# A hybrid trunk layer on one core: four-tile visits for the second modulation, two late groups, one-operation table levels, and first loads in another order

## The chip, the cores and the metric

The kernel runs on one core of a Trainium2 chip. The metric is the device time of one execution in microseconds (us), as the median over several runs. One further execution was recorded by the hardware profiler; all rows below come from it.

The engines are named as in the trace: PE multiplies matrices (PEld is its weight load), DVE works on vectors, ACT applies functions and copies, POOL is the general engine, and SP issues nearly all loads, in the order of its program.

## The reference

```python
cond = silu(c)                                   # c: 1 x 2048
mod = cond @ w_mod + b_mod                       # 2048 x 12288
sh1, sc1, gt1, sh2, sc2, gt2 = split(mod, 6)
h = rms_norm(x, g_pre_mix) * (1 + sc1) + sh1     # x: 256 x 2048
y = hybrid_mixer(h, ...)   # h @ w_in, then three branches:
      # SSM of 2048 complex states with a GLU, dilated attention of 24 heads,
      # a gated short convolution; each is projected to 2048 columns, scaled by a
      # sigmoid gate of h @ w_in, summed, and multiplied by w_o
x = x + gt1 * rms_norm(y, g_post_mix)
h = rms_norm(x, g_pre_ffn) * (1 + sc2) + sh2
y = conv_ffn(h, ...)       # h @ w_up (11264 columns), width-3 convolution, silu(a) * b, @ w_down
x = x + gt2 * rms_norm(y, g_post_ffn)
```

All values are float32. Half 0 of the modulation is the pair (sh1, sc1), half 1 the pair (sh2, sc2).

## The kernel before

**Products.** Each float32 operand is split in a high and a low part: ACT copies the high one (L72), DVE subtracts for the low one (L73). `mm3` (L125 to L128) makes three matmuls of one product. Weights come as tiles of 128x1024 (512 KB) into the four slots of the pool `raw`; `next_weights` keeps two tiles loaded and split ahead of the one in use (`AHEAD = 2`). A slot is free for the next load when both halves of the split have read it.

**Stages, in time from the span's start.** Start (to 48.7 us): load `x` transposed as `xt` in four tiles, spread `silu(c)` over all partitions (`cond_row`, two tiles), sum the squares of `xt` on PE (`ssps`), take the root on ACT and the reciprocal with a Newton step on DVE (`rstd`), make the modulation of the first two column groups, and from them `h` and its split, `hh` and `hl` (`h_pair`). Then four passes of two column groups over `w_in` for SSM and attention (`inps`, to 285 us), the convolution branch (`cps`, to 386 us), three gate branches of 16 output tiles `f` each (`gps`: branch 0 and 1 to about 660 us, then the GLU, branch 2 from about 690 to 787 us), the output projection (`ops<-mh`, to 876 us), a middle part that normalises and transposes (to 892 us), the FFN's upward products (`ups`, to 1390 us) and its second output projection (to 1637 us).

**Modulation.** Each half has eight groups of 256 scale and 256 shift columns. A group on DVE (`mod_half`) reads eight 128x1024 weight tiles; each is multiplied with `cond_row` and summed by one operation (L193). Half 0 puts its tiles in the pool `bo` (six slots, two of them held by `cond_row` and two at first by the loaded `c`), half 1 in `raw`, that is, among the weights. `PE_MOD` names the groups made on PE instead (groups 4 to 7 of half 1): `mod_rows_pe` takes two tiles, one in `mraw` and one in `raw`, for four matmuls of 32x512 output (L154) between the matmuls of the main work. We call this a visit. A group has four visits, and then a transposition on PE (L177) and a sum on DVE. The post-mix gate is made by `mod_gate`, whose tiles go into the pool `dx` (five slots).

**Order of the work.** Side work is written as generators; a `Filler` steps each by a rate per tick, two ticks in an `f`. The order of each engine's program is that in which these steps fall. In the convolution and in gate branches 0 and 1, `fs` is the SSM and `m2` the second modulation: groups 0 to 3 as DVE rows, then 4 to 7 as visits. `mod_gate` runs in gate branch 2 and in the output projection.

**SSM tables.** `table` makes cosine and sine rows `T` of 256 steps by four doublings for each of 16 state blocks: one scaled copy on ACT (L700) and two operations on DVE (L703, L707) in each. The angles come from POOL operations in `ssm_params`, at the start.

## Time and profile before

| what | value |
|---|---|
| median of three runs (1638.06, 1642.01, 1641.61) | 1641.61 us |
| the profiled execution | 1646.62 us |
| its span, first to last instruction | 1644.6 us |
| PE busy | 97% of the span |
| DVE, ACT, POOL busy | 74%, 50%, 3% |
| bytes moved by DMA | 388.52 MB, mean 236 GB/s |

The span is what the views below are drawn over; about 2 us of the execution lie outside it. A busy share is over the whole span and says nothing of a single stage.

### The profile page before, as it was taken

Reading aid. Unit: us, or ns where it says so; the run is one execution under the profiler, and the core shown is the slowest. Engines: PE = TensorE matmul, PEld = TensorE weight load, DVE = VectorE, ACT = ScalarE, POOL = GpSimd, SP = SyncE. Lnnn points to the kernel's source line nnn. Section 1 sums busy time; section 2 is a strip of 40 time slices with the busy share of each in tenths; the row PEclk is TensorE's granted clock in tenths of the full one; section 3 lists DMA queues with packets and bytes.
Section 4 is the critical chain, followed back from the end, with each engine's and each line's share of the span. In section 5 each row is a group of like instructions: output and inputs, shape, how many; then the busy total and the mean of one; then the engine's idle time right before and its main releaser. Section 6 shows DMA issues by size and latency. Waiting matters only on the chain.

```text
span 1644.6 us, 26089 instructions
## 1 busy us (share of the span) xinstructions
PE 1587.6 (97%) x10112; PEld 1400.8 (85%) x10112; DVE 1217.2 (74%) x1854; ACT 814.7 (50%) x1223; POOL 52.0 (3%) x102
## 2 busy tenths in 40 slices
PE   5899999999999999999998999999999999999997
PEld 3898998889888889999887888888888888888886
DVE  5889987887777788787757778877788777444444
ACT  4553434664445554544446555555555555343342
POOL 8021000000000000000000000000000000000000
PEclk8899999999999999999999999999999999999999
DMA  7988975777776665888864777767777665556563
GB/s 264 367 316 281 372 264 172 252 252 251 266 269 240 211 230 165 299 304 321 291 200 137 227 238 235 232 215 231 235 236 230 201 190 188 185 191 191 187 188 125
DMA packets 107120, 388.52 MB, mean 236 GB/s; under 512 B 11890, under 2 KB 12018, under 8 KB 106996
## 3 DMA queue, kind: packets, MB, share of 16 engines
q1 hardware_dynamic: 105268, 380.96, 69.5%
q10 hardware_dynamic: 1728, 5.90, 1.0%
q8 instruction: 79, 1.29, 0.3%
q14 instruction: 45, 0.37, 0.1%
HBM read 384.71 MB, written 2.10 MB: 235 GB/s over the span
## 4 chain that ended last, share of the span: by engine, by line
PE 81%; DVE 8%; DMA 7%; ACT 3%; issue 2%; SPq 0%; DVEq 0%; ACTq 0%
PE ups L901 20%; PE ups L902 10%; PE ops L127 7%; PE ops L126 7%; PE ops L128 7%; PE gps L126 5%; PE gps L128 5%; PE gps L127 5%; PE inps L126 4%; PE inps L128 4%; PE inps L127 4%; DVE lo L73 3%; DMA raw<-in_wB 2%; DMA raw<-in_wmod_t 2%; DMA raw<-in_wA 1%
## 5 line engine op out<-in xcount | busy, mean ns | idle before, releaser
L73 DVE TENSOR_TENSOR lo<-raw,hi 128x1024 fp32r<-128x1024 f32 x520 | 635.4, 1225 | 290.1 <-ACT hi L72 287.8
L72 ACT CAST hi<-raw 128x1024 fp32r<-128x1024 f32 x520 | 543.0, 1047 | 555.2 <-PE ops L128 172.9
L901 PE MATMUL ups<-h2p,hi 128*128 128x512 f32 x1408 | 495.3, 394 | 0.1
L902 PE MATMUL ups<-h2p,lo 128*128 128x256 f32 x1408 | 398.1, 283 | 0.0
L901 PEld LDWEIGHTS ups<-h2p,hi 128*128 128x128 f32 x1408 | 264.4, 188 | 61.6 <-ACT hi L72 0.5
L902 PEld LDWEIGHTS ups<-h2p,lo 128*128 128x128 f32 x1408 | 264.7, 188 | 0.6 <-issue 0.5
L128 PE MATMUL gps<-hh,lo 128*128 128x256 f32 x768 | 217.2, 283 | 4.1 <-DVE lo L73 4.1
L126 PE MATMUL gps<-hh,hi 128*128 128x256 f32 x768 | 220.0, 286 | 0.2 <-ACT hi L72 0.2
L127 PE MATMUL gps<-hl,hi 128*128 128x256 f32 x768 | 216.8, 282 | 0.0
L126 PEld LDWEIGHTS gps<-hh,hi 128*128 128x128 f32 x768 | 145.5, 189 | 15.7 <-issue 8.9
L128 PEld LDWEIGHTS gps<-hh,lo 128*128 128x128 f32 x768 | 145.3, 189 | 4.9 <-DVE lo L73 4.9
L126 PE MATMUL inps<-hh,hi 128*128 128x256 f32 x448 | 128.1, 287 | 22.1 <-ACT hh L72 14.8
L127 PEld LDWEIGHTS gps<-hl,hi 128*128 128x128 f32 x768 | 145.4, 189 | 0.2 <-issue 0.2
L126 PE MATMUL ops<-hi,ah 128*128 128x512 f32 x352 | 138.9, 395 | 0.0
L127 PE MATMUL ops<-lo,ah 128*128 128x512 f32 x352 | 138.9, 395 | 0.0
L128 PE MATMUL ops<-hi,al 128*128 128x512 f32 x352 | 138.9, 395 | 0.0
L128 PE MATMUL inps<-hh,lo 128*128 128x256 f32 x448 | 128.2, 287 | 1.9 <-DVE lo L73 1.7
L127 PE MATMUL inps<-hl,hi 128*128 128x256 f32 x448 | 127.4, 285 | 0.3 <-DVE hl L73 0.3
L126 PEld LDWEIGHTS inps<-hh,hi 128*128 128x128 f32 x448 | 85.9, 193 | 22.9 <-ACT hh L72 15.2
L128 PEld LDWEIGHTS inps<-hh,lo 128*128 128x128 f32 x448 | 85.6, 191 | 3.2 <-DVE lo L73 3.1
L127 PEld LDWEIGHTS inps<-hl,hi 128*128 128x128 f32 x448 | 86.0, 192 | 0.8 <-DVE hl L73 0.6
L193 DVE SCALAR_TENSOR_TENSOR mraw<-mraw,cond_row 128x1024 f32<-128x1024 f32 x64 | 79.1, 1254 | 0.7 <-DMA mraw<-in_wmod_t 0.6
(248 smaller groups left out, 2325.8 us busy)
## 6 DMA issues: line engine op xcount, KB each, us to landing
raw<-in_wup SPq DMA_DIRECT2D x176, 512.0 KB, 4.2
raw<-in_wB SPq DMA_DIRECT2D x120, 512.0 KB, 4.6
raw<-in_wdn SPq DMA_DIRECT2D x88, 512.0 KB, 3.5
raw<-in_wA SPq DMA_DIRECT2D x80, 512.0 KB, 5.2
mraw<-in_wmod_t SPq DMA_DIRECT2D x64, 512.0 KB, 5.9
raw<-in_wmod_t SPq DMA_DIRECT2D x32, 512.0 KB, 4.8
dx<-in_wmod_g SPq DMA_DIRECT2D x32, 512.0 KB, 6.7
raw<-in_wo SPq DMA_DIRECT2D x32, 512.0 KB, 4.5
```

Source lines behind the costliest of these rows:

```text
L72: marks["act"] = nc.scalar.copy(hi, src)
L73: nc.vector.tensor_sub(lo, src, hi)
L126: nc.tensor.matmul(dst, wh, ah, start=first, stop=False)
L127: nc.tensor.matmul(dst, wh, al, start=False, stop=False)
L128: nc.tensor.matmul(dst, wl, ah, start=False, stop=last)
L193: nc.vector.scalar_tensor_tensor(w, w, 1.0, cond_row[kc], ALU.mult, ALU.mult, accum_out=mp2[:, q, kc : kc + 1])
L901: nc.tensor.matmul(ps, wh[:, c], hp, start=kt == 0, stop=False)
L902: nc.tensor.matmul(ps[:, 0], wl[:, c], hp[:, 0], start=False, stop=kt == KT - 1)
```

## The change

Five edits are made together.

1. `PE_MOD` of half 1 is (3, 4, 5) instead of (4, 5, 6, 7). A PE group is now made in two visits of eight matmuls: four tiles per visit, of which two come in halves into four tiles `mq` (in the pool `uv`, whose space the SSM's `M1` and `M2` give up: six buffers each instead of eight), one into `mraw`, one into `raw`. There is a step of the generator after each tile.
2. Half 1 is called in three pieces: groups 0 to 2 during the convolution, groups 3 to 5 during gate branches 0 and 1 at a rate of 1 step per `f`, groups 6 and 7 as DVE rows during gate branch 2 (a quarter step per `f`) and, behind `mod_gate`, in the output projection (`rest`), where what is left is drained before the last quarter.
3. `table` scales the two rows of `T` in two ACT operations, one with the negated sine (`NPS`), and needs one DVE operation for each doubling.
4. The angles become a generator in three parts: the reciprocal of the denominator first, the rest after the root and after the first `h`.
5. The first loads are asked for in another order: `c` in four pieces of 512, the first modulation group's tiles between those of `xt`, two weight tiles ahead of the second group's.

```diff
@@ -27,7 +27,7 @@
 GATE_ORDER = (2, 1, 0)
 AHEAD = 2
 LAG = False
-PE_MOD = ((), (4, 5, 6, 7))
+PE_MOD = ((), (3, 4, 5))
 
 V_C = 0
 V_GPM = 16
@@ -144,20 +144,28 @@
         return w
 
     def mod_rows_pe(src_of, res):
-        condp = marks["condp"]
+        condp, quarter = marks["condp"], marks["quarter"]
         ps = psA.tile([P, 512], F32, tag="A", name="modps")
-        for j in range(4):
-            ws = [mod_raw(i, src_of(2 * j + i)) for i in range(2)]
-            yield
-            for q in range(4):
-                kt = 4 * j + q
+        for j in range(2):
+            parts = []
+            for i in range(4):
+                src = src_of(4 * j + i)
+                if i < 2:
+                    for k in range(2):
+                        t = quarter[2 * i + k]
+                        nc.sync.dma_start(t, src[:, 512 * k : 512 * k + 512])
+                        parts.append(t)
+                else:
+                    w = mod_raw(i, src)
+                    parts += [w[:, 0:512], w[:, 512:1024]]
+                yield
+            for q in range(8):
+                kt = 8 * j + q
+                c = kt % 4
                 nc.tensor.matmul(
-                    ps[32 * q : 32 * q + 32], condp[:, kt],
-                    ws[q // 2][:, 512 * (q % 2) : 512 * (q % 2) + 512],
+                    ps[32 * c : 32 * c + 32], condp[:, kt], parts[q],
                     start=kt < 4, stop=kt >= KT - 4,
                 )
-            if j < 3:
-                yield
         acc = sp.tile([P, 512], F32, tag="junk", name="acc")
         nc.scalar.copy(acc, ps)
         res.append(acc)
@@ -286,6 +294,8 @@
                 for t in range(2):
                     mms(j, w, t)
             last = [next_weights(min(AHEAD, nj - 1 - j)) for j in range(cut, nj)]
+            if filler is not None and n == 2:
+                filler.finish()
             if n == 2:
                 dummy = cp.tile([P, 1], F32, tag="dummy", name="dummy")
                 nc.scalar.activation(dummy, ss[:, 0, 0:1], AF.Sqrt)
@@ -312,9 +322,17 @@
...
-        def ssm_params():
+        params = []
+
+        def ssm_angles():
             AR, AI = V[:, V_AR : V_AR + 16], V[:, V_AI : V_AI + 16]
             dt, th, kk, t1, t2, mag = (sm(n) for n in ("dt", "th", "kk", "t1", "t2", "mag"))
+            rden = sm("rden")
+            nc.gpsimd.tensor_mul(rden, AR, AR)
+            nc.gpsimd.tensor_mul(t2, AI, AI)
+            nc.gpsimd.tensor_add(rden, rden, t2)
+            nc.vector.reciprocal(rden, rden)
+            yield
...
@@ -328,6 +346,7 @@
...
             nc.gpsimd.tensor_scalar(th, th, 3.1415925, -3.1415925, ALU.min, ALU.max)
+            yield
...
@@ -338,24 +357,22 @@
...
-            nc.gpsimd.tensor_mul(t1, AR, AR)
-            nc.gpsimd.tensor_mul(t2, AI, AI)
-            nc.gpsimd.tensor_add(t1, t1, t2)
-            nc.vector.reciprocal(t1, t1)
...
+            NPS = mp.tile([P, 4, 16], F32, tag="NPS", name="NPS")
+            nc.gpsimd.tensor_scalar(NPS, PS[:, 4:8], -1.0, None, ALU.mult)
...
@@ -393,7 +410,8 @@
...
-        mag, PC, PS, SC, SS, fr, fi = ssm_params()
+        angles = ssm_angles()
+        next(angles)
         nc.scalar.activation(cond, V[:, V_C : V_C + KT], AF.Silu)
         ident = mp.tile([P, P], F32, tag="ident", name="ident")
...
@@ -404,20 +422,23 @@
...
-        c1 = [mp.tile([1, 1024], F32, tag="bo", name="c1", bufs=6) for _ in range(2)]
-        for i in range(2):
-            nc.sync.dma_start(c1[i], crow[:, 1024 * i : 1024 * i + 1024])
+        c1 = [mp.tile([1, 512], F32, tag="uv", name="c1", bufs=20) for _ in range(4)]
+        for i in range(4):
+            nc.sync.dma_start(c1[i], crow[:, 512 * i : 512 * i + 512])
...
         xt = [big("xt") for _ in range(4)]
-        for i in range(4):
-            nc.sync.dma_start(xt[i], xT[:, 4 * i : 4 * i + 4])
+        first = mod_half(0, 0, scale1, shift1, V_GPM, V_BMOD + 16, V_BMOD, LAG)
+        for i in range(7):
+            next(first)
+            if i >= 3:
+                nc.sync.dma_start(xt[i - 3], xT[:, 4 * (i - 3) : 4 * (i - 3) + 4])
+        drain(first)
...
@@ -428,10 +449,12 @@
                     ps[:, :S], oinv, sq[:, k], start=(i + k == 0), stop=(i + k == 8)
                 )
         rstd = tp.tile([P, S], F32, tag="rstd", name="rstd")
-        nc.scalar.activation(rstd, ps[:, :S], AF.Sqrt, bias=eps[:, 0:1])
+        root = nc.scalar.activation(rstd, ps[:, :S], AF.Sqrt, bias=eps[:, 0:1])
         nc.vector.reciprocal(rstd, rstd)
         nt = tp.tile([P, S], F32, tag="nt", name="nt")
         newton(rstd, nt, ps[:, :S])
+        with tc.issue_after(root.ins):
+            next(angles)
 
         hhq = [big("hh", F32R) for _ in range(4)]
         hlq = [big("hl", F32R) for _ in range(4)]
@@ -579,7 +602,12 @@
...
         fa = Filler(attention_all(), 0.0)
-        drain(prepare(GROUPS[0]))
+        h_pair(0)
+        with tc.issue_after(marks["act"].ins):
+            drain(angles)
+        mag, PC, PS, NPS, SC, SS, fr, fi = params[0]
+        prefetch(2)
+        drain(prepare(GROUPS[0][1:]))
         for gi, grp in enumerate(GROUPS):
             n = len(grp)
             nxt = GROUPS[gi + 1] if gi + 1 < len(GROUPS) else []
@@ -686,8 +714,8 @@
             gqh = mp.tile([P, 4, S], F32R, tag="bo", name="gqh", bufs=6)
             gql = mp.tile([P, 4, S], F32R, tag="bo", name="gql", bufs=6)
             ssm_st["g"] = (gq, gqh, gql)
-            M1s = [mp.tile([P, 2, S], F32, tag="uv", name="M1", bufs=20) for _ in range(8)]
-            M2s = [mp.tile([P, 2, S], F32, tag="uv", name="M2", bufs=20) for _ in range(8)]
+            M1s = [mp.tile([P, 2, S], F32, tag="uv", name="M1", bufs=20) for _ in range(6)]
+            M2s = [mp.tile([P, 2, S], F32, tag="uv", name="M2", bufs=20) for _ in range(6)]
             Ts = {}
 
             def table(s):
@@ -698,14 +726,13 @@
                     m = 1 << e
                     tt = zp.tile([P, 2, P], F32, tag="tt", name="tt", bufs=2)
                     nc.scalar.activation(
-                        tt[:, :, :m], T[:, :, :m], AF.Copy, scale=PS[:, e, s : s + 1]
+                        tt[:, 0, :m], T[:, 1, :m], AF.Copy, scale=NPS[:, e - 4, s : s + 1]
+                    )
+                    nc.scalar.activation(
+                        tt[:, 1, :m], T[:, 0, :m], AF.Copy, scale=PS[:, e, s : s + 1]
                     )
                     nc.vector.scalar_tensor_tensor(
-                        T[:, 0, m : 2 * m], T[:, 0, :m], PC[:, e, s : s + 1], tt[:, 1, :m],
-                        ALU.mult, ALU.subtract,
-                    )
-                    nc.vector.scalar_tensor_tensor(
-                        T[:, 1, m : 2 * m], T[:, 1, :m], PC[:, e, s : s + 1], tt[:, 0, :m],
+                        T[:, :, m : 2 * m], T[:, :, :m], PC[:, e, s : s + 1], tt[:, :, :m],
                         ALU.mult, ALU.add,
                     )
                 Ts[s] = T
...
@@ -802,20 +829,23 @@
...
-        def mods2():
-            for g in range(8):
+        def mods2(groups):
+            for g in groups:
                 yield from mod_half(1, g, scale2, shift2, V_GPF, V_BMOD + 64, V_BMOD + 48)
 
         fill = lambda g: Filler(g, 0.0)
-        m2 = fill(mods2())
+        m2 = fill(mods2((0, 1, 2)))
         run(conv_branch(), (fa, 3.1), (m2, 2))
         fa.finish()
+        m2.finish()
...
+        marks["quarter"] = [mp.tile([P, 512], F32, tag="uv", name="mq", bufs=20) for _ in range(4)]
         fs = fill(ssm_all(zp))
-        run(gate_branch(0, 2), (fs, 0.7), (m2, 2))
-        run(gate_branch(1, 1), (fs, 0.75), (m2, 1.5))
+        m2 = fill(mods2((3, 4, 5)))
+        run(gate_branch(0, 2), (fs, 0.7), (m2, 1.0))
+        run(gate_branch(1, 1), (fs, 0.75), (m2, 1.0))
         fs.finish()
         m2.finish()
         zs.close()
@@ -831,8 +861,15 @@
             return w
 
         mg = fill(mod_gate(0, gg, load_late, 3))
-        run(gate_branch(2, 0), (mg, 1.5))
-        mg.rate = 1.0
+        m2 = fill(mods2((6, 7)))
+        run(gate_branch(2, 0), (mg, 1.4), (m2, 0.25))
+
+        def rest():
+            yield from gen_g
+            yield from gen_m
+
+        gen_g, gen_m = mg.gen, m2.gen
+        mg = Filler(rest(), 1.0)
 
         ss = cp.tile([P, 2, 4], F32, tag="ss", name="ss1", bufs=2)
         x1 = []
```

On DVE's program at the start, the rows from the reciprocal `rstd` to the first `scale1` are these in the kernel before (L193 multiplies a modulation tile, `mp2_302` is group 0, `mp2_338` group 1):

```order
L432 RECIPROCAL rstd_262<-rstd_262 128x256
L193 SCALAR_TENSOR_TENSOR mraw_315,mp2_302<-mraw_315,cond_row_207 128x1024
L193 SCALAR_TENSOR_TENSOR mraw_318,mp2_302<-mraw_318,cond_row_214 128x1024
L193 SCALAR_TENSOR_TENSOR mraw_321,mp2_302<-mraw_321,cond_row_207 128x1024
L193 SCALAR_TENSOR_TENSOR mraw_324,mp2_302<-mraw_324,cond_row_214 128x1024
L446 TENSOR_TENSOR h_331<-xt_221,rstd_262 128x512
L198 TENSOR_REDUCE mf_301<-mp2_302 128x4
L193 SCALAR_TENSOR_TENSOR mraw_339,mp2_338<-mraw_339,cond_row_207 128x1024
L201 SCALAR_TENSOR_TENSOR scale1_74<-mf_301,vec_67 128x2
L205 TENSOR_TENSOR shift1_75<-mf_301,vec_67 128x2
L193 SCALAR_TENSOR_TENSOR mraw_342,mp2_338<-mraw_342,cond_row_214 128x1024
L204 TENSOR_TENSOR scale1_74<-scale1_74,vec_67 128x2
```

After the change (L201 is the same operation; `mp2_133` is group 0, `mp2_357` group 1, `mp2_431` a group of the next pass), the rows from group 0's last tile, then those from group 1's last tile on:

```order
L201 SCALAR_TENSOR_TENSOR mraw_159,mp2_133<-mraw_159,cond_row_121 128x1024
L206 TENSOR_REDUCE mf_132<-mp2_133 128x4
L209 SCALAR_TENSOR_TENSOR scale1_74<-mf_132,vec_67 128x2
L213 TENSOR_TENSOR shift1_75<-mf_132,vec_67 128x2
L212 TENSOR_TENSOR scale1_74<-scale1_74,vec_67 128x2
L453 RECIPROCAL rstd_199<-rstd_199 128x256
L201 SCALAR_TENSOR_TENSOR mraw_358,mp2_357<-mraw_358,cond_row_114 128x1024
L266 SCALAR_TENSOR_TENSOR nt_202<-rstd_199 128x256
L73 TENSOR_TENSOR lo_347<-raw_344,hi_346 128x1024
L267 SCALAR_TENSOR_TENSOR ssps_166<-ssps_166,nt_202 128x256
```

```order
L201 SCALAR_TENSOR_TENSOR mraw_379,mp2_357<-mraw_379,cond_row_121 128x1024
L73 TENSOR_TENSOR lo_401<-raw_398,hi_400 128x1024
L206 TENSOR_REDUCE mf_356<-mp2_357 128x4
L201 SCALAR_TENSOR_TENSOR mraw_432,mp2_431<-mraw_432,cond_row_114 128x1024
L209 SCALAR_TENSOR_TENSOR scale1_74<-mf_356,vec_67 128x2
L213 TENSOR_TENSOR shift1_75<-mf_356,vec_67 128x2
L201 SCALAR_TENSOR_TENSOR mraw_461,mp2_431<-mraw_461,cond_row_121 128x1024
L212 TENSOR_TENSOR scale1_74<-scale1_74,vec_67 128x2
```

All eight tiles of group 0 now stand ahead of the reciprocal, where four of them stood behind it; two tiles of the next pass and the splits of four weight tiles (`lo`, two of them in the rows left out) now stand ahead of the last operation on group 1's scale.

On PE, in gate branch 0, a visit reads so before (the rows around it are the main work):

```order
L127 MATMUL gps_4618<-bol_2956,hi_4621 128x256
L128 MATMUL gps_4618<-boh_2955,lo_4622 128x256
L154 MATMUL modps_4694<-mraw_4695,condp_198 32x512 x2
L154 MATMUL modps_4694<-raw_4697,condp_198 32x512 x2
L126 MATMUL gps_4748<-hh_269,hi_4627 128x256
L127 MATMUL gps_4748<-hl_273,hi_4627 128x256
```

After the change:

```order
L127 MATMUL gps_4605<-bol_2963,hi_4608 128x256
L128 MATMUL gps_4605<-boh_2962,lo_4609 128x256
L165 MATMUL modps_4307<-mq_4220,condp_101 32x512
L165 MATMUL modps_4307<-mq_4221,condp_101 32x512
L165 MATMUL modps_4307<-mq_4222,condp_101 32x512
L165 MATMUL modps_4307<-mq_4223,condp_101 32x512
L165 MATMUL modps_4307<-mraw_4525,condp_101 32x512 x2
L165 MATMUL modps_4307<-raw_4603,condp_101 32x512 x2
L126 MATMUL gps_4735<-hh_219,hi_4614 128x256
L127 MATMUL gps_4735<-hl_223,hi_4614 128x256
```

The visit has eight matmuls instead of four, and there are 6 of them instead of 16.

On SP, in the output projection, the loads in the kernel before are those of the output weights alone:

```order
L66 DMA raw_9417<-in_wo 128x1024
L66 DMA raw_9435<-in_wo 128x1024
L66 DMA raw_9453<-in_wo 128x1024
L66 DMA raw_9471<-in_wo 128x1024
L66 DMA raw_9489<-in_wo 128x1024
L66 DMA raw_9507<-in_wo 128x1024
```

After the change, at the same place:

```order
L66 DMA raw_9390<-in_wo 128x1024
L66 DMA raw_9396<-in_wmod_t1 128x1024
L66 DMA raw_9415<-in_wo 128x1024
L66 DMA raw_9423<-in_wmod_t1 128x1024
L66 DMA raw_9438<-in_wo 128x1024
L66 DMA raw_9444<-in_wmod_t1 128x1024
L66 DMA raw_9459<-in_wo 128x1024
L66 DMA raw_9465<-in_wmod_t1 128x1024
L66 DMA raw_9480<-in_wo 128x1024
L66 DMA raw_9486<-in_wmod_t1 128x1024
```

Twelve modulation tiles stand one by one between the output weights' tiles, in the same four slots; four more stand in gate branch 2.

## Rows read from the trace of the kernel before

**Rows 1.** The page, parts 1 and 4: busy shares; chain that ended last.

```profile
PE 1587.6 (97%) x10112; PEld 1400.8 (85%) x10112; DVE 1217.2 (74%) x1854; ACT 814.7 (50%) x1223; POOL 52.0 (3%) x102
...
PE 81%; DVE 8%; DMA 7%; ACT 3%; issue 2%; SPq 0%; DVEq 0%; ACTq 0%
```

**Rows 2.** The page, part 5: costliest groups (count, busy us, mean ns, idle before).

```profile
L73 DVE TENSOR_TENSOR lo<-raw,hi 128x1024 fp32r<-128x1024 f32 x520 | 635.4, 1225 | 290.1 <-ACT hi L72 287.8
L72 ACT CAST hi<-raw 128x1024 fp32r<-128x1024 f32 x520 | 543.0, 1047 | 555.2 <-PE ops L128 172.9
...
L193 DVE SCALAR_TENSOR_TENSOR mraw<-mraw,cond_row 128x1024 f32<-128x1024 f32 x64 | 79.1, 1254 | 0.7 <-DMA mraw<-in_wmod_t 0.6
```

**Rows 3.** Timeline of PE, first 52 us: start, duration, operation, [idle before].

```profile
3.96 7.16 PE L415 MATMUL crps<-c,ones 1*128 1x512 f32 x8 [3.96 <-DMA c<-in_crow]
...
13.76 9.24 PE L427 MATMUL ssps<-sq,oinv 128*128 128x256 f32 x28 [0.64 <-ACT sq L425]
37.83 0.80 PE L126 MATMUL inps<-hh,hi 128*128 128x256 f32 x2 [14.82 <-ACT hh L72]
...
48.71 0.58 PE L126 MATMUL inps<-hh,hi 128*128 128x256 f32 x1 [7.25 <-ACT hi L72]
```

**Rows 4.** Timeline of ACT, first 60 us.

```profile
23.04 0.47 ACT L431 ACTIVATE rstd<-ssps,eps 128x256 f32<-128x256 f32 x1 [0.60 <-PE ssps L427]
```

**Rows 5.** Timeline of DVE, first 60 us.

```profile
23.55 1.75 DVE L432 RECIPROCAL rstd<-rstd 128x256 f32<-128x256 f32 x1 [1.92 <-ACT rstd L431]
...
46.07 0.16 DVE L204 TENSOR_TENSOR scale<-scale,vec 128x2 f32<-128x2 f32 x1
```

**Rows 6.** The tile mraw, first 45 us: DMA from issue to landing.

```profile
DMA to landing us min/median/max: 3.4/4.8/9.3
```

**Rows 7.** inps by windows: length, busy PE PEld DVE ACT, clock, DMA, GB/s.

```profile
48.60:53.86 5.26, 5.15 (x23) 5.11 (x24) 0.00 (x0) 0.00 (x0) 0.50 1.02 404
53.86:61.10 7.24, 7.24 (x63) 7.24 (x63) 0.00 (x0) 1.78 (x3) 1.00 0.98 372
```

**Rows 8.** Timeline of PE around one visit in gate branch 0.

```profile
426.01 0.28 PE L128 MATMUL gps<-boh,lo 128*128 128x256 f32 x1
426.22 0.62 PE L154 MATMUL modps<-mraw,condp 128*32 128x512 f32 x2
...
426.68 0.60 PE L154 MATMUL modps<-mraw,condp 128*32 128x512 f32 x2
...
427.22 0.39 PE L126 MATMUL gps<-hh,hi 128*128 128x256 f32 x1
```

**Rows 9.** Waits on PE, 424 to 660 us: total us, times, longest.

```profile
PE modps L154 <- DMA mraw<-in_wmod_h: 4.4, 4, 1.3
```

**Rows 10.** Waits of all engines, 386 to 424 us.

```profile
DVE raw L193 <- DMA raw<-in_wmod_t: 8.3, 5, 4.1
...
PE gps L128 <- DVE lo L73: 2.5, 3, 1.3
```

**Rows 11.** Groups by form, 386 to 660 us (busy us, mean ns, idle before).

```profile
L700 ACT ACTIVATE tt<-T,PS 128x32 f32<-128x32 f32 x15 | 4.8, 318 | 0.3
...
L703 DVE SCALAR_TENSOR_TENSOR T<-T,PC,tt 128x16 f32<-128x16 f32 x16 | 3.6, 227 | 0.0
```

**Rows 12.** Timeline of PE in the output projection.

```profile
795.00 0.39 PE L127 MATMUL ops<-lo,mh 128*128 128x512 f32 x1
...
797.72 0.39 PE L127 MATMUL ops<-lo,mh 128*128 128x512 f32 x1
```

**Rows 13.** DMA issues, 785 to 820 us: count, KB each, median us to landing.

```profile
raw<-in_wo SPq DMA_DIRECT2D x13, 512.0 KB, 4.8
dx<-in_wmod_g SPq DMA_DIRECT2D x4, 512.0 KB, 6.8
```

**Rows 14.** DMA issues, 820 to 876 us.

```profile
raw<-in_wo SPq DMA_DIRECT2D x14, 512.0 KB, 3.6
```

**Rows 15.** All work by window, gate 2's end (columns as rows 7, POOL too).

```profile
785.00:795.00 10.00, 10.00 (x55) 8.66 (x54) 10.00 (x11) 4.99 (x6) 0.00 (x0) 1.00 1.00 386
```

More of the change, by code (lines that the diff above doesn't have):

```diff
@@ L347, in ssm_params @@
             nc.gpsimd.tensor_add(fr, fr, t2)
-            nc.gpsimd.tensor_mul(fr, fr, t1)
+            nc.gpsimd.tensor_mul(fr, fr, rden)
             nc.gpsimd.tensor_mul(fi, li, AR)
@@ L351, in ssm_params @@
             nc.gpsimd.tensor_sub(fi, fi, t2)
-            nc.gpsimd.tensor_mul(fi, fi, t1)
+            nc.gpsimd.tensor_mul(fi, fi, rden)
             for j in range(7):
@@ L376, in ssm_params @@
                 nc.gpsimd.tensor_add(b2, b2, t)
-            return mag, PC, PS, SC, SS, fr, fi
+            params.append((mag, PC, PS, NPS, SC, SS, fr, fi))
         def ssm_out():
@@ L412 @@
             for j in range(2):
-                c = slice(512 * j, 512 * j + 512)
                 ps = psA.tile([P, 512], F32, tag="A", name="crps")
-                nc.tensor.matmul(ps, ones[0:1], c1[i][:, c], start=True, stop=True)
-                nc.scalar.activation(cr[:, c], ps, AF.Silu)
+                nc.tensor.matmul(ps, ones[0:1], c1[2 * i + j], start=True, stop=True)
+                nc.scalar.activation(cr[:, 512 * j : 512 * j + 512], ps, AF.Silu)
             cond_row.append(cr)
         xt = [big("xt") for _ in range(4)]
-        for i in range(4):
-            nc.sync.dma_start(xt[i], xT[:, 4 * i : 4 * i + 4])
+        first = mod_half(0, 0, scale1, shift1, V_GPM, V_BMOD + 16, V_BMOD, LAG)
[4 more added lines that the diff above has]
+        drain(first)
         ps = psB.tile([P, 512], F32, tag="B", name="ssps")
@@ L732, in ssm_all @@
                     ts_ = T[:, 1].unsqueeze(1).to_broadcast([P, 2, S])
-                    M1, M2 = M1s[s % 8], M2s[s % 8]
+                    M1, M2 = M1s[s % 6], M2s[s % 6]
                     mm.append((M1, M2))
```

## The prediction, made before the changed kernel had run

> **What bounds the kernel now.** I read the busy shares and the chain that ended last first. PE is busy 97% of the span, and the chain lies on PE for 81%; DVE (8%), DMA (7%) and ACT (3%) hold the rest [rows 1]. So time can be won in two ways only: PE gets less to do, or one of its pauses gets shorter. What DVE or ACT save by themselves counts only where PE waits for them.
>
> The next views were PE's timeline and its waits, stage by stage, to find the pauses that the change touches. There are three. At the start PE stands still for 14.82 us until the first `hh`, does 12 matmuls, and stands still again for 7.25 us, until 48.71 [rows 3]; the last thing missing is group 1's scale, ready on DVE at 46.07 [rows 5]. Around the beginning of gate branch 0, PE waits 2.5 us for `lo` from DVE, while DVE itself waits 8.3 us for modulation tiles [rows 10]. In gate branches 0 and 1 the visits wait 4.4 us for their tiles [rows 9].
>
> **Fewer visits.** Around a visit of four matmuls, the last matmul of the main work starts at 426.01 and the next at 427.22 [rows 8]. Without a visit the spacing there is 0.12 us (that of neighbouring `gps` matmuls), so the visit costs 1.21 - 0.12 = 1.09 us. Its two pairs of rows start at 426.22 and 426.68: two tiles side by side cost 0.46 us for two matmuls each, and what is left is the change from and to the main work. A visit of eight matmuls has two such passes more: 1.09 + 2 x 0.46 = 2.01 us. Before: 16 x 1.09 = 17.4 us. After: 6 x 2.01 = 12.1 us. That is **-5.3 us**. Group 3 comes to PE, and groups 6 and 7 leave it; both are in the counts (three groups of two visits for four groups of four).
>
> **Waits at the visits.** Before, a visit's tiles are asked for half an `f` ahead; after, a step stands after each tile at one step per `f`, so that the last tile has a whole `f` to land in and the first one four; an `f` takes 8.6 us there (32 of them from 386 to 660). Tiles landed in 3.4 to 9.3 us where the queue was fullest, 4.8 in the median [rows 6]. A whole `f` covers nearly all of that. I take all of the 4.4 us [rows 9]: **-4.4 us**, bounds 0 and -4.4.
>
> **Gate branch 0's first tiles.** The stall goes: group 3 is no longer made by DVE there, so no modulation tile sits in DVE's program ahead of a `lo`. **-2.5 us** [rows 10], bounds 0 and -2.5. What becomes late next is the tables' work, and nothing on PE waits for it within this stretch.
>
> **The start.** The quantity to follow is the time X at which group 1's scale is ready. Before, DVE's reciprocal starts at 23.55 and X is 46.07, so the list between took 22.5 us [rows 5]. After, that list has two modulation rows fewer (2 x 1.25), four `lo` more (4 x 1.225) [rows 2], one `h` less (some 0.7), and group 0's four small operations stand ahead of it (some 0.5). POOL's angles no longer run beside it, which I estimate at -1.5 with the waits. That gives 22.5 - 2.5 + 4.9 - 0.7 - 0.5 - 1.5 = 22.2 us. The root that opens the list ended at 23.04 + 0.47 = 23.5 [rows 4]. After, xt2 and xt3 are asked for behind six and seven modulation tiles, and those wait for slots that DVE frees at 1.25 us a row; `cond_row` is complete only after PE's spreading of `c`, at 11.1 [rows 3]. Three rows end at about 15.4, then tile 6 and xt3 are issued, and with 4.8 us [rows 6] xt3 is there at 20.2. Its two squares follow at PE's pace of 9.24 / 7 = 1.32 us each [rows 3], and the root ends at about 24.0. So X = 24.0 + 22.2 = 46.2, as late as before. But 24 instead of 12 matmuls of the first pass are done by then, since weights for both halves are there. Before, the pass went on from 48.71 with 24 at the half clock (0.50) and some 60 at full clock in 7.24 us [rows 7], 0.12 each; 12 fewer are worth 1.4 us. The result is 46.2 - 46.1 - 1.4 = -1.3; I take **-1 us**. Bounds: +4, where a load or ACT's `hi` holds one of the four `lo` that now stand ahead of X, and everything behind it on DVE waits with it (X at 50, from 2 landings of 3.4 to 4.8 each half hidden); -5.5, the rival below. PE's work from 54 us on is continuous enough in these windows that a shift of the start carries through.
>
> **The tables.** DVE loses 64 operations of at least 0.23 us, ACT gains 64 of about 0.32 us [rows 11]. No PE row waits for a table in this view, and ACT is busy only half the time [rows 1], so the cover is the SSM's slack within `f`. **0**, bounds -2 and +2 (the spread if one in ten were uncovered, 64 x 0.32 / 10).
>
> **Four late tiles in gate branch 2.** DVE's eight `raw` rows held up PE for 2.5 us [rows 10], 0.3 each; **+1 us**, bounds 0 and +1.2.
>
> **Twelve late tiles in the output projection.** PE uses a weight tile in 12 matmuls, 795.00 to 797.72, so 2.72 us [rows 12]. After, each weight tile has a modulation tile beside it in the four slots. A slot is filled in L, the time from issue to landing, and held for about 2.5 us more by `hi`, `lo` (1.05 + 1.23) or the modulation row [rows 2]. Two pairs are under way at once, so a pair takes (L + 2.5) / 2. Above 2.72 us PE falls back by the difference, 12 times, less the lead of two tiles (5.4 us). L = 3.6, as in the later part before [rows 14], loses nothing. L = 4.3 loses 12 x 0.68 - 5.4 = 2.8; L = 4.8, as in the first part [rows 13], 5.8. Twice the bytes should bring L between these: **+3 us**, bounds 0 and +5.8, with the 6.8 us of `dx` [rows 13] as a rival. Queued behind a late row on DVE are the weights' `lo`, and PE waits for those.
>
> A rate could bound this place too. Two tiles, 1.05 MB in 2.72 us, are 385 GB/s; in a stretch with DMA busy throughout the trace shows 386 [rows 15], and 404 and 372 at the start [rows 7]. So it just fits. The Trainium skill's page "DMA: Bandwidth & Descriptors", section Specifications, gives about 358 GB/s as a core's limit from HBM; by it a pair would take 2.93 us, an estimate, and the twelve 2.5 us more. The trace does not agree with it: all three stretches are above.
>
> **Sum.** -5.3 - 4.4 - 2.5 - 1 + 0 + 1 + 3 = -9.2 us. The profiled execution took 1646.6 and would take 1637.4. It is 5 us above the median of the runs, 1641.6; carried over to that, 1632.4, so **1632 us**.
>
> **Rivals.**
> 1. *The four slots bind.* L is 4.8 us or a little more in the output projection, and the late tiles in gate 2 cost as much again: -9.2 + 3 to +8, so 1635 to 1641, about 1638. For it: SP's program alternates the two kinds there. Against: 3.6 us in the later part.
> 2. *The start gives more.* Table loads for the angles no longer stand between ACT's first squares. If loads keep up, PE's 32 `ssps` matmuls follow the spreading at once: 11.1 + 8 x 1.32 = 21.7, the root at 22.2, X at 44.4. With 1.4 for the twelve matmuls and 2.3 for a clock that is up before the second half (24 x (0.215 - 0.12)), that is 46.1 - 44.4 + 3.7 = 5.4 instead of 1: 1628, between 1625 and 1629. Against: xt3's place in SP's order.
> 3. *The waits only move.* The visits wait for the last of four tiles as they did for one of two, and DVE's stall at gate 0 turns up at another row: 4.4 + 2.5 less, 1639.
> 4. *Slower: landings in the output projection like those of `dx`.* The sum without that term is -12.2; it becomes slower by 0.3%, 4.9 us, when the term exceeds 17.1, that is 12 x ((L + 2.5) / 2 - 2.72) > 22.5, L above 6.7. At 7.3 the term is 20.8 and the time 1650. For it: `dx` took 6.8 us beside the same weights [rows 13]; against: `mod_gate` asks for three of its tiles ahead, the late rows for one at a time.
> 5. *A rate binds it.* At the lowest of the rates, 372 GB/s, a pair takes 2.82 us and twelve lose 1.2 more: 1633.6. By the Trainium skill's figure ("DMA: Bandwidth & Descriptors", Specifications) it would be 1635, an estimate.
>
> **How the numbers follow.** About 0.3%, 4.9 us, is what a measurement of this kernel can tell from no change: below 1636.7 is faster, above 1646.5 slower. Chances: the forecast 0.44 (1629 to 1637), rival 1 0.18 (a quarter of it faster), rival 2 0.14, rival 3 0.11, rival 4 0.10, rival 5 0.03. Faster: 0.44 + 0.04 + 0.14 + 0.03 = 0.65; the same: 0.14 + 0.11 = 0.25; slower 0.10. From 1624 to 1642 all but rival 4 and the edges of the others are held, a little over 8 in 10.
>
> **What would show it.** In the profile after: visits 2.0 us apart from the main work, with under 1 us of waits for `mq`, `mraw` or `raw`; no PE wait for `lo` at gate 0's first tiles; 24 matmuls of `inps` before the second pause, and that pause ending near 48 to 49; in the output projection, `raw` landing in about 4.3 us and PE waiting some 3 us for `lo`. If the visits wait as before, or the output projection takes over 95 us instead of some 89, or the second pause at the start ends after 51, the prediction is wrong at that step.

## The result, and the profile after

The changed kernel takes **1631.47 us** (median of five runs, 1627.32 to 1634.02) against 1642.01 (1638.06 to 1643.91): a ratio of 0.9936, with a 95% interval of 0.9915 to 0.9957. The forecast was 1632 us. The profiled execution took 1632.77 us with a span of 1631.0.

The page's parts 1 and 4, as in [rows 1]:

```profile
PE 1580.3 (97%) x10076; PEld 1397.4 (86%) x10076; DVE 1212.6 (74%) x1806; ACT 821.9 (50%) x1284; POOL 71.9 (4%) x103
...
PE 82%; DVE 7%; DMA 6%; issue 2%; ACT 2%; SPq 0%; DVEq 0%; ACTq 0%
```

These shares look as before. Where the time went shows only in the lengths of the stages, which I take from PE's timeline. Their bounds are the starts of first or last matmuls of a kind: the last `inps` (since the span's start), the first `gps`, the last `gps` of branch 1 and of branch 2, the first and last `ops<-mh`, the first `ups`, and the last matmul of all.

| | last `inps` | conv | gates 0, 1 | GLU, gate 2 | `ops<-mh` | middle | rest |
|---|---|---|---|---|---|---|---|
| before | 284.7 | 101.3 | 273.6 | 127.5 | 88.6 | 16.3 | 743.0 |
| after | 280.7 | 102.2 | 256.3 | 124.2 | 98.9 | 16.2 | 743.0 |
| difference | -4.1 | +1.0 | -17.3 | -3.3 | +10.3 | -0.2 | 0.0 |

The sum, before rounding, is -13.5 us. The two spans differ by 13.6, the medians by 10.5: the profiled execution of before was 4.6 us above its median, that of after 1.3. About 3.7 us of this can be placed. The kernel gate_rate_alone (below), whose code is that of before up to gate branch 2, has its last `inps` at 282.9 and takes 271.8 us for gate branches 0 and 1, about 1.9 less than before in each. The differences -4.1 and -17.3 hold that much of the one profile's lateness.

**The visits.** PE's timeline around the first visit, the counterpart of [rows 8]:

```profile
418.32 0.28 PE L128 MATMUL gps<-boh,lo 128*128 128x256 f32 x1
418.53 1.07 PE L165 MATMUL modps<-mq,condp 128*32 128x512 f32 x8
419.42 0.60 PE L165 MATMUL modps<-mraw,condp 128*32 128x512 f32 x2
...
420.39 0.39 PE L126 MATMUL gps<-hh,hi 128*128 128x256 f32 x1
```

From the start of the main work's last matmul to that of its next it is 2.07 us, 1.95 beyond the spacing of 0.12. In PE's waits from 383 to 640 us no row is left at all, where before it waited 4.4 us for tiles [rows 9] and 2.5 for `lo` [rows 10].

**The start.** PE's timeline, the counterpart of [rows 3], and ACT's, with the two late squares and the root (before, the root started at 23.04 [rows 4]):

```profile
12.44 5.25 PE L448 MATMUL ssps<-sq,oinv 128*128 128x256 f32 x16 [1.21 <-ACT sq L446]
...
36.00 0.79 PE L126 MATMUL inps<-hh,hi 128*128 128x256 f32 x2 [10.52 <-ACT hh L72]
...
49.08 1.01 PE L126 MATMUL inps<-hh,hi 128*128 128x256 f32 x3 [5.80 <-ACT hh L72]
```

```profile
20.24 1.15 ACT L446 ACTIVATE sq<-xt 128x512 f32<-128x512 f32 x2 [4.99 <-DMA xt<-in_xT]
22.80 1.15 ACT L446 ACTIVATE sq<-xt 128x512 f32<-128x512 f32 x2 [1.41 <-DMA xt<-in_xT]
...
25.52 0.47 ACT L452 ACTIVATE rstd<-ssps,eps 128x256 f32<-128x256 f32 x1 [0.26 <-PE ssps L448]
```

ACT waits for xt2 (4.99 us) and xt3 (1.41 us), and the root starts 2.5 us later than before. On DVE (beside [rows 5]) the list behind it takes 21.1 us:

```profile
26.02 1.75 DVE L453 RECIPROCAL rstd<-rstd 128x256 f32<-128x256 f32 x1 [0.16 <-ACT rstd L452]
...
47.09 0.16 DVE L212 TENSOR_TENSOR scale<-scale,vec 128x2 f32<-128x2 f32 x1
```

Work on `inps` by windows, beside [rows 7]: the clock comes up about a microsecond earlier.

```profile
49.00:53.00 4.00, 3.92 (x17) 3.83 (x18) 0.00 (x0) 0.00 (x0) 0.50 1.03 419
53.00:59.70 6.70, 6.70 (x58) 6.70 (x57) 0.00 (x0) 1.79 (x3) 0.99 0.49 175
```

**The output projection.** PE's timeline where the last late tiles stand, ACT's and SP's at the same place, the windows over them, and the DMA issues from 764 to 863 us (beside [rows 13] and [rows 14]):

```profile
840.07 0.39 PE L128 MATMUL ops<-hi,ml 128*128 128x512 f32 x1
843.04 0.50 PE L126 MATMUL ops<-hi,mh 128*128 128x512 f32 x1 [2.57 <-ACT hi L72]
844.30 0.50 PE L127 MATMUL ops<-lo,mh 128*128 128x512 f32 x1 [0.76 <-DVE lo L73]
...
845.16 0.63 PE L127 MATMUL ops<-lo,mh 128*128 128x512 f32 x1
845.59 0.63 PE L128 MATMUL ops<-hi,ml 128*128 128x512 f32 x1
```

```profile
841.94 1.04 ACT L72 CAST hi<-raw 128x1024 fp32r<-128x1024 f32 x1 [4.32 <-DMA raw<-in_wo]
```

```profile
830.62 0.33 SPq L66 DMA_DIRECT2D raw<-in_wo  x1
831.76 3.46 SPq L66 DMA_DIRECT2D raw<-in_wmod_t  x3
837.61 8.49 SPq L66 DMA_DIRECT2D raw<-in_wo  x6
```

```profile
838.00:846.00 8.00, 4.67 (x17) 3.20 (x16) 7.09 (x14) 2.49 (x3) 0.00 (x0) 0.94 0.84 285
846.00:850.00 4.00, 4.00 (x14) 3.19 (x13) 2.45 (x2) 2.31 (x3) 0.00 (x0) 0.70 0.77 284
```

```profile
raw<-in_wo SPq DMA_DIRECT2D x28, 512.0 KB, 5.1
raw<-in_wmod_t SPq DMA_DIRECT2D x12, 512.0 KB, 4.6
```

For nine pairs PE waits little: 0.4 us for `lo` at 831 us, 0.8 at 837. Then the rows that are left are drained: three modulation tiles stand one behind the other on SP ahead of an output weight and hold three of the four slots. That weight is asked for at 837.61 us, ACT waits 4.32 us for it, PE stands still for 2.57 us, and after that the granted clock falls to its lower level for a time (0.70 in the mean over 846 to 850), where neighbouring matmuls stand 0.43 us apart. From the stop to 849 us the stage loses some 5.4 us so.

A second loss is spread over the whole stage, with the clock at 1.00. Twelve matmuls span 2.80 us here, and spanned 2.72 before [rows 12]:

```profile
794.10 0.39 PE L127 MATMUL ops<-lo,mh 128*128 128x512 f32 x1
...
796.90 0.39 PE L127 MATMUL ops<-lo,mh 128*128 128x512 f32 x1
```

That is 0.2333 us for one instead of 0.2267, 2.5 us over the stage's 384.

### The profile page after: what moved, and what is told of

It reads as the page before. It is cut to its first block, busy times and chain, and to the rows that moved or that the text cites. A ratio compares the mean times of both kernels' runs of the same rounds, so it can differ in the third digit from the quotient of the medians.

```text
span 1631.0 us, 26004 instructions
## 1 busy us (share of the span) xinstructions
PE 1580.3 (97%) x10076; PEld 1397.4 (86%) x10076; DVE 1212.6 (74%) x1806; ACT 821.9 (50%) x1284; POOL 71.9 (4%) x103
## 4 chain that ended last, share of the span: by engine, by line
PE 82%; DVE 7%; DMA 6%; issue 2%; ACT 2%; SPq 0%; DVEq 0%; ACTq 0%
PE ups L938 20%; PE ups L939 10%; PE gps L126 6%; PE gps L128 6%; PE gps L127 6%; PE ops L127 5%; PE ops L128 5%; PE ops L126 5%; PE inps L126 4%; PE inps L128 4%; PE inps L127 4%; DVE lo L73 3%; DMA raw<-in_wo 2%; DMA mraw<-in_wmod_t 2%; DMA raw<-in_wmod_t 1%
## 5 line engine op out<-in xcount | busy, mean ns | idle before, releaser
L126 PE MATMUL inps<-hh,hi 128*128 128x256 f32 x448 | 128.4, 288 | 16.3 <-ACT hh L72 16.3
L226 DVE SCALAR_TENSOR_TENSOR acc<-raw,cond,acc 128x1024 f32<-128x1024 f32 x32 | 41.1, 1284 | 71.1 <-DMA raw<-in_wmod_g 69.9
L201 DVE SCALAR_TENSOR_TENSOR mraw<-mraw,cond_row 128x1024 f32<-128x1024 f32 x64 | 78.3, 1241 | 19.7 <-DMA mraw<-in_wmod_t 18.8
```

What stands on the lines that cost most here:

```text
L126: nc.tensor.matmul(dst, wh, ah, start=first, stop=False)
L201: nc.vector.scalar_tensor_tensor(w, w, 1.0, cond_row[kc], ALU.mult, ALU.mult, accum_out=mp2[:, q, kc : kc + 1])
L226: nc.vector.scalar_tensor_tensor(acc, ws.pop(0), cond[:, kt : kt + 1], acc, ALU.mult, ALU.add)
```

## The experiments

All ratios are to the kernel before, run beside on the same chip. The stages are read from one profiled execution of each kernel; the same code differs by up to 1.9 us in a stage between two of them (273.6 and 271.8 above).

| kernel | median us | ratio, 95% | last `inps` | gates 0, 1 | GLU, gate 2 | `ops<-mh` |
|---|---|---|---|---|---|---|
| after | 1631.47 | 0.9936 (0.9915 to 0.9957) | 280.7 | 256.3 | 124.2 | 98.9 |
| late_half_rate | 1627.48 | 0.9917 (0.9901 to 0.9933) | 280.9 | 256.3 | 127.7 | 91.0 |
| late_in_dx | 1623.29 | 0.9889 (0.9874 to 0.9904) | 279.5 | 256.3 | 124.2 | 91.0 |
| old_places | 1633.15 | 0.9946 (0.9930 to 0.9962) | 280.5 | 257.1 | 125.4 | 101.7 |
| visits_of_four | 1632.86 | 0.9942 (0.9922 to 0.9961) | 279.9 | 257.9 | 125.1 | 98.8 |
| start_as_before | 1634.40 | 0.9956 (0.9940 to 0.9973) | 282.5 | 257.1 | 125.0 | 97.9 |
| tables_two_ops | 1629.23 | 0.9925 (0.9898 to 0.9951) | 280.6 | 256.3 | 124.2 | 97.2 |
| gate_rate_alone | 1640.79 | 0.9988 (0.9976 to 1.0000) | 282.9 | 271.8 | 124.7 | 88.6 |
| new_visits_old_plan | 1635.30 | 0.9960 (0.9944 to 0.9976) | 282.4 | 263.3 | 126.0 | 88.6 |
| dx_aligned_all | 1623.11 | 0.9876 (0.9860 to 0.9892) | 280.0 | 257.1 | 124.7 | 89.3 |
| dx_aligned_mh | 1621.62 | 0.9860 (0.9844 to 0.9877) | 279.9 | 256.4 | 124.5 | 89.9 |

**late_half_rate**, from the changed kernel:

```diff
-        run(gate_branch(2, 0), (mg, 1.4), (m2, 0.25))
+        run(gate_branch(2, 0), (mg, 1.4), (m2, 0.5))
```

> The changed kernel with the late rows at half a step per f in gate branch 2 instead of a quarter: eight of the sixteen tiles are done there, eight alternate with the output weights, and none is left to be drained in a row. Theory (the drain): of the 10.3 us that the output projection lost against before (98.9 against 88.6), some 6.6 are the stall of PE from 836 to 848 us, where the last modulation tiles are asked for one behind the other ahead of the next output weight, with the half clock that follows it. They go; the output projection takes 91.5 to 93, and gate branch 2 at most 1 us more: 5 to 7 us less than the changed kernel, about 1625. Rival (the slots bind at every pair): eight pairs in place of twelve give back a third of the loss, 2 to 4 us, and PE waits in many places of about 0.3 us.

The drain theory held: the output projection takes 91.0 us, and PE waits nowhere in it; the eight pairs themselves cost nothing. tables_two_ops agrees, which does the same work here as the changed kernel: the drain is the only place at which PE waits. The price of the half rate came elsewhere: in gate branch 2 PE now waits 3.8 us for `lo`, and that stage is 3.5 us longer, not at most 1. So the median fell by 4 us and not by 5 to 7. PE's waits from 640 to 860 us:

```profile
PE gps L128 <- DVE lo L73: 3.8, 3, 2.3
```

**late_in_dx**, from the changed kernel:

```diff
-                        w = raw_tile(wmod_t[half][i, 2 * q + kc])
+                        w = marks.get("late", raw_tile)(wmod_t[half][i, 2 * q + kc])
...
+        marks["late"] = load_late
         mg = fill(mod_gate(0, gg, load_late, 3))
```

> The changed kernel with the sixteen late tiles in the five slots dx instead of the four slots raw; the order of SP's program stays. Theory (the drain): the output weights keep their four slots and are asked for on time whatever the order of the last rows, the stall at 836 to 848 goes: 5 to 7 us less than the changed kernel, the output projection at 91.5 to 93. Rival (order on SP and DVE): what delays the weight is its place behind the modulation tiles in SP's program, and on DVE the rows ahead of lo, not the slot; the stall stays within 2 us of what it was.

The output projection falls to 91.0 us with gate branch 2 as in the changed kernel. PE is busy through the place of the old stall, at a granted clock of 1.00, though the weights land only 0.3 us sooner than in the changed kernel and the modulation tiles 1.0 us later (windows, then DMA issues from 762 to 852 us):

```profile
761.00:800.00 39.00, 39.00 (x169) 30.82 (x168) 35.03 (x37) 19.50 (x24) 0.00 (x0) 1.00 0.94 364
...
826.00:838.00 12.00, 12.00 (x53) 9.69 (x52) 9.85 (x15) 6.49 (x10) 0.00 (x0) 1.00 0.64 237
838.00:853.00 15.00, 15.00 (x66) 11.87 (x64) 8.94 (x15) 7.10 (x11) 0.00 (x0) 1.00 0.64 231
```

```profile
raw<-in_wo SPq DMA_DIRECT2D x27, 512.0 KB, 4.8
dx<-in_wmod_t SPq DMA_DIRECT2D x12, 512.0 KB, 5.6
```

Output weights and modulation tiles stand in the same order on SP, the last three tiles in a row too, so the rival falls: what held up the weight was the slot that it had to wait for.

**old_places**, from the changed kernel, the order of allocation alone, by which some slots also rotate (the later allocations of these names go):

```diff
-            rden = sm("rden")
+            rden = tp.tile([P, 16], F32, tag="rden", name="rden")
+            PC = mp.tile([P, 8, 16], F32, tag="PC", name="PC")
+            PS = mp.tile([P, 8, 16], F32, tag="PS", name="PS")
+            lr, li, fr, fi = (sm(n) for n in ("lr", "li", "fr", "fi"))
+            SC = mp.tile([P, 16, 16], F32, tag="SC", name="SC")
+            SS = mp.tile([P, 16, 16], F32, tag="SS", name="SS")
...
+        crs = [mp.tile([P, 1024], F32, tag="bo", name="cond_row", bufs=6) for _ in range(2)]
         c1 = [mp.tile([1, 512], F32, tag="uv", name="c1", bufs=20) for _ in range(4)]
```

> The changed kernel with the tables PC, PS, SC, SS and the tiles cond_row asked for ahead of the pieces of c, so that the pools bo and uv lie where they lay before (mh and ml from byte 155264 of a partition on instead of 127424); all work and its order stay, but for a rotation of slots. Theory (place): the output projection's matmuls follow each other at 0.2335 us where they did at 0.2267 before, with the granted clock at 1.00 in both, because mh and ml lie elsewhere; 384 of them make 2.6 us. At the old place 0.2267 comes back and 2 to 3 us with it, less up to 0.9 us in the gates, where boh gained (0.1178 against 0.1198). Rival (traffic): the slower pace comes from the loads beside it, and stays at 0.233.

The pace of 0.227 came back, and the time did not: the output projection took 101.7 us. With the slots binding, a faster PE can only wait longer for them: PE waits 5.3 us for `lo` and 1.8 for `hi`, where it waited 1.9 and 2.6 in the changed kernel. The stage became 2.8 us longer and not just as long; part of it is a longer stretch at the lower clock behind the drain (846.1 to 852.9 us, in the changed kernel 845.0 to 848.4), and the rest is open. The gates lost 0.7 us, of up to 0.9 that were expected.

**dx_aligned_all** and **dx_aligned_mh** ask the same question with the slots out of the way. From late_in_dx, the first line for both, the second for dx_aligned_mh alone:

```diff
-            rden = sm("rden")
+            rden = tp.tile([P, 16], F32, tag="rden", name="rden")
...
-        c1 = [mp.tile([1, 512], F32, tag="uv", name="c1", bufs=20) for _ in range(4)]
+        c1 = [mp.tile([1, 512], F32, tag="uv", name="c1", bufs=20) for _ in range(4)]; sm("pad")
```

> The kernel late_in_dx with one buffer of 64 bytes moved to another pool, so that everything behind it in the pool mix lies 64 bytes lower: mh and ml at 384 instead of 448 modulo 2048, boh and bol too; the order of all instructions is the same. Theory (alignment): the matmuls of the output projection follow at 0.2333 where mh and ml lie 64 bytes off a multiple of 128, and at 0.2267 where they lie on one, whatever the region; the output projection falls from 90.97 to about 88.5 us, while boh, now on a multiple of 128, costs 0.7 us in gate branches 0 and 1 (256.3 to 257.0) and some 0.3 in branch 2: 1.5 us less in all, about 1622. Rival (region): the faster pace belongs to the addresses above 155264; it stays at 0.2333 and the time at 1623.

> As dx_aligned_all, with a gap of 64 bytes behind the pool's buffers uv, so that mh and ml lie on a multiple of 128 and boh and bol 64 bytes off one, as in late_in_dx. Theory (alignment): the output projection at 88.5 us, gate branches 0 and 1 at 256.3: 2.5 us less than late_in_dx, about 1621. Rival (region): no difference, 1623.

Moving `mh` and `ml` by 64 bytes is enough (dx_aligned_mh, PE's timeline, again twelve matmuls, 2.72 us):

```profile
790.37 0.39 PE L127 MATMUL ops<-lo,mh 128*128 128x512 f32 x1
...
793.09 0.39 PE L127 MATMUL ops<-lo,mh 128*128 128x512 f32 x1
```

The pace is 0.227 in both, in the region where it was 0.2333, so that the region falls and the alignment stands. In the gates the effect is the other way round and smaller, as expected: 257.1 us with `boh` on a multiple of 128, 256.4 with `boh` 64 bytes off. Of 2.5 us expected in the output projection 1.6 came in dx_aligned_all and 1.1 in dx_aligned_mh; one short wait for `lo` in each (0.4 and 0.7 us), with what follows it, took up most of the rest. By the ratios' intervals the two kernels can hardly be told from late_in_dx: the pace is shown matmul by matmul, its worth in the whole time is not. dx_aligned_mh has the lowest ratio of this study, 0.9860 against the changed kernel's 0.9936.

**visits_of_four**: the changed kernel with the function `mod_rows_pe` of the kernel before (and without the tiles `mq`).

> The changed kernel with the visits as before, four matmuls and two tiles each, for the same three groups at the same rate: 12 visits of four instead of 6 of eight. Theory (price and lead apart): the visits cost 12 x 1.2 instead of 6 x 2.1 us, so 1.8 us more than the changed kernel; the waits for tiles stay away, because at one step per f both tiles have a whole f to land in: 1 to 3 us more in all. Rival (the four tiles make the lead): with two tiles per visit some of the visits wait again as they did before, 4 us in all, and the time is 5 to 6 us above the changed kernel.

Gate branches 0 and 1 take 1.6 us more (257.9), and PE has no wait there: the price as expected, and no need of four tiles at this rate.

**new_visits_old_plan**: the kernel before with the changed `mod_rows_pe`, the tiles `mq`, and six buffers for `M1` and `M2`.

> The kernel before with visits of eight matmuls and four tiles, for its four groups at its rates of 2 and 1.5 steps per f, and M1, M2 with six buffers. Theory (price and lead apart): 8 visits of 2.1 us instead of 16 of 1.2, so 2.4 us less; the last tile still has half an f to land in, so that 2 to 4 of the 5.6 us of waits stay, and the 3.8 us that PE waits for lo at the beginning of gate branch 0 stay: gate branches 0 and 1 fall from 273.6 to 268 to 271. Rival (the four tiles make the lead): the waits go too, 265 to 266.

Here my theory fell. The branches took 263.3 us, 10.3 less than before, more even than the rival's 265; at the old rates no wait for a tile is left. All of PE's waits from 383 to 650 us:

```profile
PE gps L128 <- DVE lo L73: 1.1, 2, 0.7
```

So it is not the whole `f` alone that takes the waits away. In this kernel one tile is asked for in half an `f`, before two were asked for together ahead of each visit; at half the rate two together are no harm either (visits_of_four). Both remove the waits, each without the other. Which share of it is the slot `mraw`, of which there is one, was not tried, nor what the fewer buffers of `M1` and `M2` do. That PE's waits for `lo` at the beginning of gate branch 0 also fell here, from 2.5 to 1.1 us, was not foreseen either.

**start_as_before**: the changed kernel with loads, angles and first group in the old order.

> The changed kernel with the start of the kernel before: first loads, angles and first modulation group in their old order; the rest is the change. Theory (the start gives all the lead at 285 us): the changed kernel was 1.5 us ahead when PE began the 97th matmul of inps and 4.1 us ahead at the last; the 2.6 us between came out of the second pass, where ACT waited 13.9 us for weights before and 4.8 after, because loads asked for earlier at the start left the queue shorter. Undone, the last inps matmul starts at 284 to 285 us and the time is 3 to 4.5 us above the changed kernel. Rival (only the start itself): it ends at 282 to 282.5, 1 to 2 us above.

The last `inps` matmul starts at 282.5 us, where the rival had it, and the median is 2.9 us above the changed kernel's, nearly the 3 of the theory. (The median holds more than the start: this kernel's buffers also lie elsewhere, `boh` on a multiple of 128 bytes, which old_places shows to cost 0.7 us in gate branches 0 and 1, and here they take 257.1.) Four kernels of this study have the old start: 284.7, 282.5, 282.9 and 282.4; eight have the new one: 279.5 to 280.9. Their means differ by 2.9 us (283.1 and 280.2), by 2.4 without the late 284.7. At the 97th matmul of `inps`, where the two first weight blocks end, the old start stands at 61.2, 58.5, 58.8 and 58.4 us, the new one between 58.7 and 60.3: the profiled execution of before was the late one of its kind, and the start itself gained nothing. The gain comes later, in the second pass (108 to 170 us), so the theory had its place right and the rival not. PE's waits there, before, then after:

```profile
PE inps L128 <- DVE lo L73: 1.7, 4, 0.6
PE inps L127 <- DVE lo L73: 0.7, 1, 0.7
```

```profile
PE inps L128 <- DVE lo L73: 0.6, 2, 0.5
```

All four kernels with the old start have waits of 2.4 or 2.5 us there, those with the new one none to 1.0. ACT's waits for weights in the same stretch, before, after, and in start_as_before:

```profile
ACT hi L72 <- DMA raw<-in_wA: 13.9, 8, 4.4
```

```profile
ACT hi L72 <- DMA raw<-in_wA: 4.8, 5, 2.8
```

```profile
ACT hi L72 <- DMA raw<-in_wA: 11.5, 7, 4.4
```

That the weights land earlier is thus the likely reason, but not shown: visits_of_four has the new start, ACT waits 10.0 us for weights there, and the gain came all the same.

**tables_two_ops**: the changed kernel with the old body of `table`'s loop.

> The changed kernel with two DVE operations and one ACT operation per level of a table, as before. Theory (off the path): PE waits for no table, gate branches 0 and 1 stay at 256 to 257.5 us, the time within 1 us of the changed kernel. Rival (DVE's relief counts): of the 17.4 us that gate branches 0 and 1 gained, 12.2 were foreseen; the rest came from 64 DVE operations fewer, which let lo be on time; then these branches take 259 to 262 us and the time is 3 to 5 us above the changed kernel.

Gate branches 0 and 1 take 256.3 us in both, to 0.01 us. The tables are worth nothing here. The median, 2.2 us below the changed kernel's, cannot be told from it by the intervals.

**gate_rate_alone**, from the kernel before:

```diff
-        run(gate_branch(2, 0), (mg, 1.5))
+        run(gate_branch(2, 0), (mg, 1.4))
```

> The kernel before with one number changed: mod_gate at 1.4 instead of 1.5 steps per f in gate branch 2. Theory (order on DVE): before, three operations of mod_gate stood in a row ahead of a lo, PE waited 1.79 us for it and then ran at the half clock for 3.4 us; at 1.4 only two stand there, so that gate branch 2 falls from 119.6 us to about 116.5 as in the changed kernel, and the whole to about 1638.5. Rival (loads): the weight itself landed late, and the stall stays, or moves within the branch; no change beyond 1 us.

DVE's rows of `mod_gate` that stand in a row ahead of the late `lo`, in before, then in gate_rate_alone (the changed kernel has two as well):

```profile
686.26 3.92 DVE L218 SCALAR_TENSOR_TENSOR acc<-dx,cond,acc 128x1024 f32<-128x1024 f32 x3
690.10 2.35 DVE L73 TENSOR_TENSOR lo<-raw,hi 128x1024 fp32r<-128x1024 f32 x2
```

```profile
683.91 2.60 DVE L218 SCALAR_TENSOR_TENSOR acc<-dx,cond,acc 128x1024 f32<-128x1024 f32 x2
686.43 1.22 DVE L73 TENSOR_TENSOR lo<-raw,hi 128x1024 fp32r<-128x1024 f32 x1
```

GLU and gate branch 2 take 124.7 us instead of 127.5, and PE's wait there falls as in the changed kernel (660 to 790 us, before, then gate_rate_alone):

```profile
PE gps L128 <- DVE lo L73: 1.6, 1, 1.6
```

```profile
PE gps L128 <- DVE lo L73: 0.7, 1, 0.7
```

The median moved by 1.4 us, and the ratio's interval touches 1: the place of the gain is shown, its size lies between 1.3 and 2.8 us. For new_visits_old_plan, also at 1.5, has the same three rows and a wait of 2.0 us there, and yet takes 126.0 us, 1.3 more than gate_rate_alone.

## Why the prediction was right, and where its terms were not

The time was forecast to within a microsecond, but by errors that cancel: four terms brought more than foreseen, one cost more. It took luck besides: against the profile of before, from which the terms were read, the span fell by 13.6 us and not by 9.2, and only the medians lie 10.5 apart. By its own sign, an output projection of over 95 us, the prediction was wrong at that step.

- **Fewer visits** (-5.3): right. The eight-matmul visit was put at 2.01 and measured 1.95. In the sum over PE's timeline the visits' own matmuls went from 15.9 to 11.1 us and the steps to them fell by 0.8, 5.6 together. The working left out some 0.1 us on the second matmul behind each visit (1.1 in all) and the fourth group's transposition (0.4), so that the visits brought about 7.1.
- **Waits at the visits** (-4.4) and **gate branch 0's first tiles** (-2.5): right in kind, all gone. The rest of the 17.3 us: by the starts of PE's matmuls the four waits took 4.8, the stalls for `lo` and for a branch input's low part 4.5 with the matmul behind each, and 0.8 is the main work's own pace, most of it from the place of `boh`. The reason that I gave for the waits, a whole `f` of lead, is one of two that each suffice.
- **The start** (-1): right in sign, too small, and by the wrong mechanism. Twenty-four matmuls were done by the second pause, as forecast, and that pause ended at 49.1. But the root started at 25.5, where the working's end at 24.0 means 23.5, the list behind it took 21.1 and not 22.2, and the early part gained nothing; the 2.4 to 2.9 us come from PE's waits in the second pass, which the working did not look at. It took "a shift of the start carries through" for all there was.
- **The tables** (0): right.
- **Four late tiles in gate branch 2** (+1): wrong in sign. The stage got 3.3 us shorter. The step overlooked is the rate 1.4 in place of 1.5 in the same line of the diff: it takes one of three `mod_gate` rows from ahead of a late `lo`, and with the 0.9 us that are gone from the pause that ends at 691 us went the half clock behind it (new_visits_old_plan had the pause without it). The late tiles themselves cost nothing that can be seen: gate_rate_alone, which has none there, takes 124.7 us, the changed kernel 124.2.
- **Twelve late tiles in the output projection** (+3): mis-sized. It cost 10.3 us: 7.9 of slots (98.9 against 91.0 in late_in_dx) and 2.4 of place, which the working did not know of. L was 5.1 us for the weights and not 4.3; at 5.1 the working's formula gives 12 x (3.8 - 2.72) - 5.4 = 7.6. That the figure is so near is partly luck. The loss isn't spread over the pairs: late_half_rate, with eight of them, loses none of it, and in the changed kernel some 5.4 of the 7.9 us fall on the drain of the last three tiles, most of the rest on the waits for `lo` just ahead of it.
- **The rivals.** Rival 1, the slots, was at work in the output projection (5.1 us against its "4.8 or a little more") and was outweighed; its second half, a like cost in gate branch 2, did not come. Rival 2's early root didn't come, for the reason that was given against it, xt3's place. Rival 3 fell: no wait of PE is left from 383 to 640 us. Rival 4's landings of over 6.7 us didn't come: the late tiles took 4.6 us, and 5.6 in late_in_dx, where they cost nothing. For rival 5 there is no sign: the first 39 us of that stage in late_in_dx moved 364 GB/s with PE always busy. The limit of about 358 GB/s that the Trainium skill's page "DMA: Bandwidth & Descriptors" (Specifications) gives is passed here too.

## What to carry to other kernels

When side loads share slots with the weights of the main path, look at where they end, not at their mean rate: a generator that is drained asks for its last tiles all at once, and that is where PE stops. Give such tiles slots of their own before you thin them out. And read a diff's small numbers as edits of their own: a rate changed from 1.5 to 1.4 was worth 1.3 to 2.8 us here, visits of eight matmuls in place of four 1.6.

## What was not expected of the hardware

The same f32 matmul with 512 columns, at a granted clock of 1.00, follows its neighbour at 0.2333 us where the buffers `mh` and `ml` start 64 bytes off a multiple of 128 in the partition, and at 0.2267 where they start on one: some 3%. With 256 columns and `boh` as the moving side it is the other way round, 0.1178 off and about 0.119 on. All twelve kernels of this study agree: `mh` lies on a multiple in seven of them and off it in five, `boh` on one in six and off it in six. The reason is open. A new buffer of 64 bytes anywhere ahead in a pool can thus move a stage that it has nothing to do with by 1 to 2 us. And one short pause can cost more than its length: behind the 2.57 us that end at 843 the granted clock fell to its lower level (1.2 GHz), and neighbouring matmuls stood 0.43 us apart until 848. It need not: behind the wait of 2.0 us in gate branch 2 of new_visits_old_plan the granted clock stayed at 1.00 (676 to 690 us).
